# 64 bytes of padding ahead of two groups of SBUF tiles in a one-core transformer block

## The chip, the cores and the metric

The kernel runs on one core of one Trainium2 chip. The metric is the device time of one execution in microseconds (us); lower is better. A time given without more is the median of the runs shown.

## The reference, cut to what matters

One decoder layer on 2048 tokens with a model width of 1024, in float32: a mixer with eight dilated-attention heads beside a gated linear recurrence, and a squared-ReLU MLP, each between two RMS norms.

```
h = rms_norm(x, mix_norm_pre)
z = h @ w_in                                  # 1024 -> 2560: q, k, v, recurrence input, gate
m = concat(dilated_attention(q, k, v), rg_lru(conv(xr)) * gelu(gr)) @ w_out
x = x + rms_norm(m, mix_norm_post)
h = rms_norm(x, mlp_norm_pre)
x = x + rms_norm((relu(h @ w1) ** 2) @ w2, mlp_norm_post)   # 1024 -> 4096 -> 1024
```

## The kernel before, in words

Every large product is made in three TensorE passes. Each float32 operand is split into a high part (ScalarE rounds it to the faster fp32r type, L54) and a low part (the rest, by VectorE or GpSimd, L55), and a product is high x high, low x high and high x low. So every weight tile and every activation tile exists twice, with names that end in H and L. One such pass multiplies a 128 x 128 stationary operand by a 128 x 512 moving operand; the stationary operand of the next pass is loaded (LDWEIGHTS, engine PEld in the profile) while the current moving operand streams.

The tokens are worked in two halves of 1024. The order in time is:

- **w_in (L192 to L345, about 0 to 640 us of the profile).** `Project.product` (L193 to L202) makes one 128 x 512 block z of h @ w_in by 8 x 3 passes; there are 80 such blocks. The moving operands are the tiles hH and hL (h^T, eight each for each of two blocks of 512 tokens, numbered 0 and 1). The stationary operands are wH and wL, "w_in's parts". For the first four column tiles of w_in these come from a pool of their own ("x0"), for all the others from the pool "p1", in which hH, hL and the small norm tiles lie too. The attention of the first half (L368 to L741) and the recurrence run between these products.
- **Output projection (`OutProj`, L836 to L897)** for one half; in between, `Factors.columns` (L945 to L968) transposes the normed rows to h2^T on TensorE.
- **mlp_in (L1035 to L1167).** h2^T @ w1 by a two-level scheme with seven products instead of eight: products 1 to 7 each take one factor of w1 (tiles f_1 to f_7, stationary) and one factor of h2^T (moving). Product m of a pair j of w1's column tiles is 4 x 3 = 12 passes (L1070 to L1073), and there are 16 pairs in each half. `RIGHT` (L907) says which factor of h2^T a product takes. `Factors.EARLY` are the tiles B11 (product 1), B21 (product 2) and T3 (product 7), six tiles with H and L; `Factors.LATE` are T2, T4, T1 and B22 (products 6, 4, 5, 3). The early tiles lie in the pool "hA" on the left side of SBUF, the late ones in the pool "hB" on the right. In the profile the tiles hHB11, hHB21 and hHB22 all show as hHB, and hHT1 to hHT4 as hHT; the factor f_m tells which product it is.
- **mlp_out (L1170 to L1330)** with the second half's attention woven in, then output projection, mlp_in and mlp_out of the second half.

The order on TensorE follows the program from the output projection on; before that a scheduler sets it. SBUF is laid out by pools that grow from the left or the right side; a tile that is larger or new moves what its pool allocates after it, and the pools beyond. Memory is used again by later pools, and a first write waits for the last use of what lay there before.

In the built program the places of the operands, in bytes modulo 128, are:

| moving operand | at | stationary operand | at |
|---|---|---|---|
| hH (all), hL (block 0, and k = 0, 1 of block 1) | 64 | wH, wL of the pool x0 (first 8 blocks z) | 64 |
| hL (k = 2 to 7 of block 1) | 0 | wH, wL of the pool p1 (other 72 blocks z) | 0 |
| early h2^T tiles (products 1, 2, 7) | 32 | f_1 to f_7 | 96 |
| late h2^T tiles (products 3, 4, 5, 6) | 96 | f_1 to f_7 | 96 |

Of the kernel before, what the change touches and what calls it, by code (L numbers as in the profile page):

```python
# [8 lines left out]
F32 = mybir.dt.float32  # L9
# [6 lines left out]
P = 128  # L16
# [41 lines left out]
def rsqrt_mean(nc, pool, ss, k, name, eps, e=None):  # L58

    v = e or nc.vector  # L60
    ms = pool.tile([P, k], F32, tag="rs_ms", bufs=2, name=f"ms_{name}")
    sd = pool.tile([P, k], F32, tag="rs_sd", bufs=2, name=f"sd_{name}")
    r0 = pool.tile([P, k], F32, tag="rs_r0", bufs=2, name=f"r0_{name}")
    t = pool.tile([P, k], F32, tag="rs_t", bufs=2, name=f"t_{name}")
    r = pool.tile([P, k], F32, tag="rs_r", bufs=4, name=f"r_{name}")
    nc.scalar.activation(out=sd, in_=ss, func=AF.Sqrt, scale=1.0 / D, bias=eps)
    v.tensor_scalar(out=ms, in0=ss, scalar1=-0.5 / D, scalar2=-0.5 * EPS, op0=ALU.mult, op1=ALU.add)
    nc.vector.reciprocal(out=r0, in_=sd)
    if k == 1 and e is None:
        v.scalar_tensor_tensor(out=t, in0=r0, scalar=ms, in1=r0, op0=ALU.mult, op1=ALU.mult)  # L70
    else:
        v.tensor_tensor(out=t, in0=r0, in1=ms, op=ALU.mult)
        v.tensor_tensor(out=t, in0=t, in1=r0, op=ALU.mult)
    if e is None:
        v.scalar_tensor_tensor(out=r, in0=t, scalar=1.5, in1=r0, op0=ALU.add, op1=ALU.mult)
    else:
        v.tensor_scalar(out=t, in0=t, scalar1=1.5, scalar2=None, op0=ALU.add)
        v.tensor_tensor(out=r, in0=t, in1=r0, op=ALU.mult)
    return r
# [7 lines left out]
class Project:  # L87


    def __init__(self, tc, p, pa, pl, bank, cst, scr, x, xT, g1, w_in):  # L90
        self.tc, self.nc, self.p, self.pa, self.bank, self.cst, self.scr = tc, tc.nc, p, pa, bank, cst, scr
        self.x, self.xT, self.w_in, self.pl, self.norm, self.ahead = x, xT, w_in, pl, {}, {}
        self.h, self.bc, self.lo = [None] * NBH, [None] * NBH, tc.nc.gpsimd
        self.g1 = p.tile([P, KT], F32, tag="g1", name="g1_sb")
        self.g1_d = g1
# [36 lines left out]
    def load_norm(self, tb, px=None):  # L132

        nc, p = self.nc, self.p
        n = TB // P
        parts = 1 if px else 2
        w = D // parts
        ss = p.tile([P, 2, n], F32, tag="ss", bufs=2, name=f"ss{tb}")
        for j in range(n):
            for i in range(parts):  # L140
                if px:
                    t = px.tile([P, D], F32, tag="xn", bufs=4, name=f"xn{tb}_{j}")
                else:
                    t = self.pa.tile([P, TB], F32, tag="t512", bufs=3, name=f"xn{tb}_{j}_{i}")
                nc.sync.dma_start(out=t, in_=self.x[tb * TB + j * P:tb * TB + (j + 1) * P, i * w:(i + 1) * w])
                nc.scalar.activation(out=t, in_=t, func=AF.Square, accum_out=ss[:, i, j:j + 1])
        if parts == 2:
            nc.vector.tensor_tensor(out=ss[:, 0, :], in0=ss[:, 0, :], in1=ss[:, 1, :], op=ALU.add)
        self.norm[tb] = rsqrt_mean(nc, p, ss[:, 0, :], n, f"x{tb}", self.cst["eps"], nc.gpsimd if px else None)
# [775 lines left out]
class Factors:  # L925
# [5 lines left out]
    def __init__(self, nc, sh, hf, pH):  # L931
        self.nc, self.sh, self.hf, self.H = nc, sh, hf, {}

        R = {k: sh.r(f"h2r{hf}_{k}", (P, KH, TB)) for k in ("12", "21", "11", "22")}
        self.R = [[R["11"], R["12"]], [R["21"], R["22"]]]
        self.tiles(pH, self.EARLY)

    def tiles(self, pH, names):
# [786 lines left out]
```

## Time and profile before

| what | us |
|---|---|
| median of 3 runs | 2245.89 |
| lowest and highest of them | 2237.49, 2253.74 |
| span of the profiled execution, first to last instruction | 2246.4 |
| TensorE (PE) busy in it | 2167.4 (96%) |
| VectorE (DVE) busy | 1506.9 (67%) |
| ScalarE (ACT) busy | 1230.9 (55%) |
| GpSimd (POOL) busy | 450.9 (20%) |

The profile has only the span for the execution that it recorded; what lies around the span is not shown. The span is 0.5 us above the median of the runs. A matmul's duration in the profile runs from its start to a modelled end and overlaps the next matmul, so durations of about 390 ns stand for passes that start about 230 ns apart; the starts in the timeline are the better clock. "Who waited for whom" lists idle time of an engine by what ended it. The chain of work that ended last is followed back from the end of the program, and its shares say on which engine the time was being set.

### The profile page before, as it was taken

How to read it: one execution, taken by the hardware profiler on the slowest of the kernel's cores; microseconds unless marked ns; L12 is line 12 of the kernel's file. 1: busy time of each engine (PE TensorE's matmuls, PEld its weight loads, DVE VectorE, ACT ScalarE, POOL GpSimd, SP SyncE). 2: the span in 40 equal slices, each digit the busy share in tenths (PEclk: the TensorE clock that was granted, in tenths of full speed). 3: DMA queues.
4: the chain of work that ended last, by engine and by line, in shares of the span. 5: the costliest groups of instructions: out<-in, count | busy, mean ns of one | idle time of the engine just before them, and what ended most of it. 6: DMA issues, size and time to landing. Idle time of an engine off the chain costs nothing.

```text
span 2246.4 us, 30767 instructions
## 1 busy us (share of the span) xinstructions
PE 2167.4 (96%) x10264; PEld 1774.6 (79%) x10264; DVE 1506.9 (67%) x2908; ACT 1230.9 (55%) x2489; POOL 450.9 (20%) x536
## 2 busy tenths in 40 slices
PE   8999999979999999999999999989999999999998
PEld 6678878767788788888788787778878888888887
DVE  6767465978648867675567676777766566646456
ACT  7646464655434555554666666754455555654442
POOL 5543414455223000000001111113200000000003
PEclk9999999999999999999999999999999999999999
DMA  8365684645974676878777777877553444776665
GB/s 286 100 190 176 179 242 145 183 153 163 319 255 161 221 286 242 301 265 309 223 216 221 211 237 221 234 228 225 181 189 126 169 139 164 275 236 191 193 196 179
DMA packets 224116, 473.51 MB, mean 211 GB/s; under 512 B 23428, under 2 KB 78756, under 8 KB 217684
## 3 DMA queue, kind: packets, MB, share of 16 engines
q1 hardware_dynamic: 195140, 337.52, 47.9%
q0 software_dynamic: 28816, 134.01, 16.9%
q8 instruction: 81, 1.33, 0.2%
q14 instruction: 79, 0.65, 0.1%
HBM read 337.09 MB, written 151.13 MB: 217 GB/s over the span
## 4 chain that ended last, share of the span: by engine, by line
PE 70%; DVE 10%; DMA 8%; ACT 4%; issue 3%; POOL 1%; SPq 1%; DVEq 0%; ACTq 0%; POOLq 0%
PE o L1221 8%; PE o L1222 8%; PE o L1223 8%; PE za L1072 4%; PE za L1071 4%; PE za L1073 4%; PE z L198 3%; PE z L199 3%; PE z L200 3%; PE m L858 3%; PE m L857 3%; PE m L859 3%; PE zc L1071 2%; PE zc L1072 2%; PE zc L1073 2%
## 5 line engine op out<-in xcount | busy, mean ns | idle before, releaser
L198 PE MATMUL z<-hH,wH 128*128 128x512 f32 x640 | 263.8, 412 | 15.4 <-ACT wH L54 5.7
L199 PE MATMUL z<-hL,wH 128*128 128x512 f32 x640 | 260.5, 407 | 0.3 <-DVE hL L173 0.3
L200 PE MATMUL z<-hH,wL 128*128 128x512 f32 x640 | 259.6, 407 | 0.5 <-DVE wL L55 0.5
L198 PEld LDWEIGHTS z<-hH,wH 128*128 128x128 f32 x640 | 122.9, 192 | 50.6 <-ACT wH L54 8.3
L199 PEld LDWEIGHTS z<-hL,wH 128*128 128x128 f32 x640 | 122.8, 192 | 31.2 <-issue 4.8
L200 PEld LDWEIGHTS z<-hH,wL 128*128 128x128 f32 x640 | 122.9, 192 | 30.6 <-issue 4.6
L420 ACT ACTIVATE smB<-smB,stB 128x128 f32<-128x128 f32 (+3 forms) x128 | 71.6, 560 | 90.5 <-DVE stB L414 90.2
L1076 ACT ACTIVATE sq<-sq 128x512 f32<-128x512 f32 x93 | 58.8, 632 | 92.1 <-DVE sq L1080 92.1
L55 POOL TENSOR_TENSOR wL<-wraw,wH 128x512 fp32r<-128x512 f32 x58 | 82.4, 1437 | 80.5 <-ACT wH L54 76.7
L55 DVE TENSOR_TENSOR tlB<-pT_B,thB 128x384 fp32r<-128x384 f32 x96 | 57.1, 599 | 50.4 <-ACT thB L54 47.5
L1136 POOL DMA_DIRECT2D sa<-sq x31 | 16.6, 534 | 363.9 <-ACT sq L1077 353.4
L54 ACT CAST wH<-wraw 128x512 fp32r<-128x512 f32 (+1 forms) x81 | 47.2, 612 | 65.5 <-DMA wraw<-in_dram 31.6
L420 ACT ACTIVATE sm<-sm,stA 128x256 f32<-128x256 f32 (+1 forms) x128 | 63.1, 495 | 30.3 <-DVE stA L414 29.9
L1077 ACT ACTIVATE sq<-sq 128x512 f32<-128x512 f32 x124 | 76.2, 629 | 1.8
L1255 POOL TENSOR_TENSOR y<-y,g4b 128x512 f32<-128x512 f32 x8 | 12.3, 1577 | 259.4 <-ACT junk_y L84 259.4
L414 DVE CUSTOM_DVE_ANT_0 smB<-SB,mask_b 128x128 f32<-128x128 f32 (+3 forms) x128 | 59.3, 483 | 5.7 <-PE pT_B L393 5.4
L55 DVE TENSOR_TENSOR tlA<-pT,thA 128x512 fp32r<-128x512 f32 (+1 forms) x64 | 42.4, 670 | 26.4 <-ACT thA L54 26.0
L54 ACT CAST thB<-pT_B 128x384 fp32r<-128x384 f32 x96 | 48.4, 509 | 17.8 <-PE pT_B L393 9.7
L393 PE MATMUL pT_B<-ident,smB 128*128 128x128 f32 x320 | 51.5, 276 | 2.5 <-DVE na L409 0.9
L414 DVE CUSTOM_DVE_ANT_0 sm<-S,mask_a 128x256 f32<-128x256 f32 (+1 forms) x128 | 47.5, 410 | 9.3 <-PE pT L393 4.0
L640 PE MATMUL oB<-thB,vb 128*128 128x256 f32 x192 | 46.6, 274 | 6.6 <-ACT thB L54 5.9
L1072 PE MATMUL za<-hLT,f_5H 128*128 128x512 f32 x128 | 50.0, 391 | 2.0 <-DVE hLT L55 2.0
(607 smaller groups left out, 7041.4 us busy)
## 6 DMA issues: line engine op xcount, KB each, us to landing
sa<-as POOLq DMA_DIRECT2D x31, 1024.0 KB, 6.2
w1r<-in_dram SPq DMA_DIRECT2D x56, 512.0 KB, 4.0
sa<-sq POOLq DMA_DIRECT2D x31, 768.0 KB, 4.0
wraw<-in_dram SPq DMA_DIRECT2D x79, 256.0 KB, 3.8
place<-in_dram SPq DMA_DIRECT2D x14, 1024.0 KB, 7.9
sb<-place POOLq DMA_DIRECT2D x14, 1024.0 KB, 5.3
kh<-sk SPq DMA_DIRECT2D x24, 512.0 KB, 5.0
kl<-sk SPq DMA_DIRECT2D x24, 512.0 KB, 7.1
```

The lines of the kernel that those rows point to most:

```text
L55: (lo_eng or nc.vector).tensor_tensor(out=lo, in0=src, in1=f32(hi), op=ALU.subtract))
L198: pe.matmul(z, hi[:, k, :], hh, start=(k == 0), stop=False)
L199: pe.matmul(z, hi[:, k, :], hl, start=False, stop=False)
L200: pe.matmul(z, lo[:, k, :], hh, start=False, stop=(k == KT - 1))
L414: v.tensor_tensor_reduce(out=sm[:, c0:c0 + w], in0=sp[:, c0:c0 + w], in1=mask[:, mask.shape[-1] - w:], scale=1.0, scalar=3.0e38, op0=ALU.a ...
L420: s.activation(out=sm[:, c0:c0 + w], in_=sm[:, c0:c0 + w], func=AF.Exp, scale=-1.0, bias=st[:, 0, u, cols[j]:cols[j] + 1], accum_out=st[:, ...
L1071: pe.matmul(o, hi[:, k], bh[:, k], start=start and k == 0, stop=False, skip_group_check=True)
L1072: pe.matmul(o, hi[:, k], bl[:, k], start=False, stop=False, skip_group_check=True)
L1073: pe.matmul(o, lo[:, k], bh[:, k], start=False, stop=k == KH - 1, skip_group_check=True)
L1221: pe.matmul(o, ah[:, ts], bh, start=fresh and j == 0, stop=False, skip_group_check=True)
L1222: pe.matmul(o, ah[:, ts], bl, start=False, stop=False, skip_group_check=True)
L1223: pe.matmul(o, al[:, ts], bh, start=False, stop=j == NJ - 1, skip_group_check=True)
```

## The change

Two edits. The tile `ss` (sums of squares, in the pool p1, two buffers) grows from 32 to 64 bytes for each partition, only its first half is used, and what p1 allocates after it moves up by 64 bytes. And a new tile of 64 bytes, written once by VectorE so that it exists, is allocated in the pool hA ahead of the early h2^T tiles, once in each half.

```
@@ -135,7 +135,7 @@
         n = TB // P
         parts = 1 if px else 2
         w = D // parts
-        ss = p.tile([P, 2, n], F32, tag="ss", bufs=2, name=f"ss{tb}")
+        ss = p.tile([P, 4, n], F32, tag="ss", bufs=2, name=f"ss{tb}")
         for j in range(n):
             for i in range(parts):
                 if px:
@@ -933,6 +933,7 @@
 
         R = {k: sh.r(f"h2r{hf}_{k}", (P, KH, TB)) for k in ("12", "21", "11", "22")}
         self.R = [[R["11"], R["12"]], [R["21"], R["22"]]]
+        nc.vector.memset(pH.tile([P, 16], F32, name=f"pad_h{hf}"), 0.0)
         self.tiles(pH, self.EARLY)
 
     def tiles(self, pH, names):
```

In the built program of the change, wH and wL of p1, and hL k = 2 to 7 of block 1, lie at 64 modulo 128 (hH stays at 64), and the early h2^T tiles at 96 (f stays at 96). All passes of w_in and mlp_in then have both operands at equal places. Before, 1536 of w_in's 1920 passes and 1152 of mlp_in's 2688 had them at unequal places; 216 of w_in's had both at 0. The recurrence's tiles behind p1 move from 64 to 0 together with their weights. The instructions of PE, ACT, POOL and SP keep their order; VectorE has two more. The first stands among the last splits of q, k and v of the second half (zl and vs: low parts of k and of v, zn: scaled z):

```order
 L228 TENSOR_TENSOR zn_11_1_6196<-z_11_1_6171,bc_3353 128x512
 L55 TENSOR_TENSOR vs_11_0_6167<-vt_11_0_6162,vs_11_0_6167 128x8x64
+L936 MEMSET pad_h_6273 128x16
 L55 TENSOR_TENSOR zl_7_0_6083<-zn_7_0_6080,zh_7_0_6082 128x512
 L55 TENSOR_TENSOR vs_11_1_6203<-vt_11_1_6198,vs_11_1_6203 128x8x64
 L55 TENSOR_TENSOR zl_7_1_6118<-zn_7_1_6115,zh_7_1_6117 128x512
```

Only the row with the + is new. The second stands on VectorE after the first finished row tile of the second half's output projection (xt: normed rows; nm_x, nm_m: small norm values; x: rows after the mixer); this is the change's order there:

```order
L818 SCALAR_TENSOR_TENSOR nm_x_14741<-nm_x_14741 128x1
L895 SCALAR_TENSOR_TENSOR xt_14680<-x_8_14744,nm_x_14741,g3b_0_14686 128x512
L895 SCALAR_TENSOR_TENSOR xt_14680<-x_8_14744,nm_x_14741,g3b_1_14687 128x512
L936 MEMSET pad_h_14668 128x16
L815 TENSOR_SCALAR nm_m_14830<-nm_m_14830 128x1
L816 RECIPROCAL nm_m_14830<-nm_m_14830 128x1
```

Again the memset is the only new row; neither memset waits on a semaphore. Because the early tiles sit 64 bytes higher, a few first writes in the second half wait for other former tenants: the first write of hHB21 (L54) now also waits for the store of the output rows y_6 of the first half (L1265), and the first write of hLB11 (L55) for that of y_4.

More of the change, by code (lines that the diff above doesn't have):

```diff
@@ L137, in load_norm @@
         w = D // parts
-        ss = p.tile([P, 2, n], F32, tag="ss", bufs=2, name=f"ss{tb}")
+        ss = p.tile([P, 4, n], F32, tag="ss", bufs=2, name=f"ss{tb}")
         for j in range(n):
@@ L935, in __init__ @@
         self.R = [[R["11"], R["12"]], [R["21"], R["22"]]]
+        nc.vector.memset(pH.tile([P, 16], F32, name=f"pad_h{hf}"), 0.0)
         self.tiles(pH, self.EARLY)
```

## The prediction

> **What bounds the kernel now.** I read the page first, for the engine that sets the end.
>
> ```profile
> span 2246.4 us, 30767 instructions
> PE 2167.4 (96%) x10264; PEld 1774.6 (79%) x10264; DVE 1506.9 (67%) x2908; ACT 1230.9 (55%) x2489; POOL 450.9 (20%) x536
> PE 70%; DVE 10%; DMA 8%; ACT 4%; issue 3%; POOL 1%; SPq 1%; DVEq 0%; ACTq 0%; POOLq 0%
> ```
>
> TensorE is busy nearly throughout, and 70% of the chain that ended last is its own work. The change takes no pass away. It can only change how long a pass takes, so I looked for passes of one shape that take different times. The instructions on the tiles hHB and hLT (durations are minimum, median, maximum in ns) show them:
>
> ```profile
> L1071 PE MATMUL za<-hHB,f_1H x128: 394/394/394, 730.4 to 1903.4; 128*128 128x512 f32 x128
> L1071 PE MATMUL zb<-hHB,f_2H x128: 394/394/478, 734.0 to 1906.2; 128*128 128x512 f32 x128
> L1071 PE MATMUL za<-hHB,f_3H x128: 389/389/389, 768.7 to 1930.9; 128*128 128x512 f32 x128
> L1072 PE MATMUL zc<-hLT,f_7H x128: 393/394/499, 750.1 to 1914.8; 128*128 128x512 f32 x128
> L1072 PE MATMUL zc<-hLT,f_4H x128: 389/389/397, 771.6 to 1933.9; 128*128 128x512 f32 x128
> ```
>
> The early products (f_1, f_2, f_7) take 394 ns and the late ones (f_3, f_4) 389, with no scatter to speak of: a property of the operands, not of the moment. Both kinds take f from the same pool and write the same kinds of PSUM bank; what differs is that the early moving tiles lie at 32 modulo 128 beside f at 96, and the late ones at 96. Durations end in a model, so I measure by starts. TensorE's timeline: start of an early product (zc, f_7) and of the product after it, then the same for a late one (za, f_5):
>
> ```profile
> 901.78 0.39 PE L1071 MATMUL zc<-hHT,f_7H 128*128 128x512 f32 x1
> ...
> 904.58 0.39 PE L1071 MATMUL za<-hHT,f_6H 128*128 128x512 f32 x1
> ...
> 915.58 0.39 PE L1071 MATMUL za<-hHT,f_5H 128*128 128x512 f32 x1
> ...
> 918.30 0.39 PE L1071 MATMUL za<-hHB,f_3H 128*128 128x512 f32 x1
> ```
>
> Twelve passes take 2.80 us when the places are unequal and 2.72 when they are equal: 0.08 us for a product, 6.7 ns for a pass. The same for w_in, 24 passes from a block's first row to the row after its last: one block with weights of pool x0 (both operands at 64), then four with weights of p1 (64 or 0 beside 0).
>
> ```profile
> 21.12 0.39 PE L198 MATMUL z<-hH,wH 128*128 128x512 f32 x1
> ...
> 26.57 0.39 PE L200 MATMUL z<-hH,wL 128*128 128x512 f32 x1
> ...
> 150.76 0.40 PE L198 MATMUL z<-hH,wH 128*128 128x512 f32 x1
> ...
> 156.36 0.40 PE L198 MATMUL z<-hH,wH 128*128 128x512 f32 x1
> ...
> 614.87 0.40 PE L198 MATMUL z<-hH,wH 128*128 128x512 f32 x1
> ...
> 620.38 0.39 PE L198 MATMUL z<-hH,wH 128*128 128x512 f32 x1
> ...
> 625.95 0.40 PE L198 MATMUL z<-hH,wH 128*128 128x512 f32 x1
> ...
> 631.45 0.39 PE L198 MATMUL z<-hH,wH 128*128 128x512 f32 x1
> ...
> 637.01 0.38 PE L240 MATMUL vt<-ident,zn 128*128 128x128 f32 x2
> ```
>
> 5.45 us for the equal block; 5.60, 5.51, 5.50 and 5.56 for the others, 0.05 to 0.15 more, 0.09 in the mean. The hH of the first block are the same kind of tiles at the same place as in the later ones, so it is not the moving operand's place alone.
>
> The Trainium skill ("TensorE: Matmul & The Clock Gate", section "Step-by-step: what each phase is for") speaks against this reading: it gives TensorE two independent SBUF read ports and says that loading the next weights takes no read bandwidth from the running matmul. By that, a common offset of the two operands should be worth nothing and the kernel should stay at 2246. The 394 against 389 ns above do not agree with it, and I go by them.
>
> **The change part by part.** Not every pass lies on the path that sets the end. The chain of work that ended last, by line, in three stretches: w_in and the first output projection, mlp_in of the first half, mlp_in of the second.
>
> ```profile
> by line: PE z L198 9.3%; PE z L199 9.0%; PE z L200 8.9%; issue 5.9%; PE m L858 3.9%; PE m L857 3.9%; PE m L859 3.9%; DVE xc L310 3.0%; DVE xc L331 2.2%; DMA xr<-in_dram 1.4%; DMA sw<-in_dram 1.3%; DMA woL<-swo 1.2%; DMA wraw<-in_dram 1.2%;
> ...
> by line: PE za L1072 11.9%; PE za L1071 11.8%; PE za L1073 11.7%; DMA w2x<-in_dram 8.2%; PE zc L1071 6.5%; PE zc L1072 6.4%; PE zc L1073 6.3%; issue 5.4%; DMA sa<-sq 3.1%; DMA w1r<-in_dram 2.7%; PE zb L1073 2.7%; PE zb L1071 2.6%; PE zb L10
> ...
> by line: PE za L1072 17.2%; PE za L1073 17.1%; PE za L1071 17.0%; PE zc L1073 8.7%; PE zc L1072 8.7%; PE zc L1071 8.7%; PE zb L1071 3.8%; PE zb L1072 3.8%; PE zb L1073 3.8%; DVE hLT L55 2.5%; DMA w1r<-in_dram 1.8%; PE o L1222 1.2%; PE o L12
> ```
>
> *Early products.* The rows zb are product 2 alone, always an early one, and stand for all three. In the first half they hold some 8% of 317 us (741 to 1058), 25 us of the 16 x 2.80 = 45 us that the half's product 2 needs: 57% on the path. In the second, 11.4% of 316 us (1630 to 1946), 36 of 45: 80%. There are 48 early products in each half, so 27 + 38 = 65 count, times 0.08 us: **5.2 us**. The others are hidden: in the first half the chain leaves TensorE for the loads of w2x, which keep coming late, and at both starts for the split of the late tiles (hLT), so a product that is done sooner only lengthens the wait behind it. If all 96 counted it would be 7.7; nothing excludes a gain of 0 if the wait just moves.
>
> *w_in's parts.* The z rows hold 27.2% of the first 741 us, 202 us; at 5.54 us for a block (the mean of the four) that is 36 of the 72 blocks with weights of p1. The eight blocks with weights of x0 come first, and the chain's first piece is at 91.7 us (below), after them, so all 36 are blocks that change. At the mean of 0.09 this is 3.2, at 0.15, 5.4, at 0.05, 1.8; I take **3.3 us**, near the mean, as four blocks are a small sample. All 72 at 0.15 would be 10.8. The other half of the blocks runs beside VectorE and loads that end later:
>
> ```profile
> 91.71 0.85 issue
> ...
> 562.89 8.69 DMA woL<-swo
> 575.64 8.08 DMA er<-in_dram
> 596.87 8.63 DMA sq<-zl
> 605.62 0.70 DVE zl L55
> 606.42 0.70 DVE zn L228
> ```
>
> *The memsets.* The nearest rows are the kernel's own, of 128 and of 4 columns; the new ones have 16. The third row is the wait behind the second memset's place.
>
> ```profile
> L1471 DVE MEMSET ones<- x1: 165/165/165, 0.8 to 0.8; 128x128 f32 x1
> L287 DVE MEMSET state<- x1: 62/62/62, 1.0 to 1.0; 128x4 f32 x1
> ...
> 1551.62 0.16 DVE L816 RECIPROCAL nm_m<-nm_m 128x1 f32<-128x1 f32 x1 [1.01 <-ACT nm_m L814]
> ```
>
> So each costs 0.06 to 0.17 us, nearer the small one: 0.07. The first stands ahead of zl on VectorE, which is on the chain above, so it counts; behind it wait zl and the loads of zl's store. The second falls before a wait of VectorE for ScalarE and is covered by it; without that cover it would cost the same. Together **0.1 us** lost, 0.3 at most.
>
> *Sum.* 5.2 + 3.3 - 0.1 = 8.4 us off the profiled span of 2246.4, which is 2238.0. The median of the runs is 0.5 us below that span; from 2245.9 the sum gives **2237.5 us**.
>
> *Where the wait goes next.* In mlp_in of the first half the products reach the same loads sooner, so the waits of TensorE there should grow by up to the 21 hidden products' 1.7 us; in w_in by up to 36 x 0.09 = 3.2 us.
>
> **Rivals.**
>
> *All of it arrives.* If the loads and splits that now end the waits are themselves released by TensorE's earlier work, they move with it, and every pass counts: 7.7 + 72 x 0.09 = 14.2, so **2232 us**. For it: most loads wait for a buffer that a product frees. Against it: the chain's long DMA pieces above, whose length does not shrink.
>
> *w_in gives nothing.* The differences there are small and uneven (5.50 to 5.60), and half the path is others' work; a VectorE that is always a little late would absorb the rest. Then only the 5.2 remain: **2241 us**. Against it: 36 blocks stand on the chain without a wait.
>
> *The places do not matter.* Early and late products differ in more than the place: the early ones come first in a pair, while factors of w1 are made. If that set the 394 ns, nothing changes: **2246 us**. Against it: in 128 passes the f_1H rows never leave 394, though the first two pairs load their factors ready-made. The Trainium skill's rule of two independent ports ("TensorE: Matmul & The Clock Gate", "Step-by-step: what each phase is for") would lead here.
>
> *Slower: a store that ScalarE now waits for.* The first write of hHB21 in the second half waits for the store of y_6, the third of the four at that place. Stores on L1265, ScalarE's first hHB casts, and what follows them on its queue:
>
> ```profile
> 1547.83 0.57 POOL L1265 DMA_DIRECT2D out_dram<-y  x1 [5.42 <-DMA y<-sx]
> DMA to landing us min/median/max: 4.7/5.3/10.8
> 1558.78 1.13 ACT L54 CAST hHB<-h2r 128x512 fp32r<-128x512 f32 x2
> 1561.46 0.60 ACT L882 ACTIVATE x<-m 128x512 f32<-128x512 f32 x1 [1.55 <-PE m L859]
> ```
>
> With the median 5.3 the store lands at 1553.1, 5.7 us before the cast. With the longest, 10.8, it lands at 1558.6, just in time. Only from there does it cost: queued behind the cast is L882, the square sum that the norm of the next row tile needs, with 1.55 us to spare, and after it TensorE's next output projection waits for the PSUM bank. To eat the 8.4 us gained it must land over 10 us late, 21 us after its issue, twice the longest of the eight; at 15 us late, 15 - 1.5 = 13.5 lost against 8.4 gained gives **2251 us**.
>
> **How the numbers follow.** The forecast has 0.60; all of it arrives 0.16; w_in gives nothing 0.10; no effect 0.10; the late store 0.04. The predicted time is the forecast's, 2237.5. Its own range is 2232 to 2243: the bounds of w_in (1.8 to 5.4) and some 3 us by which a median of three moves when single runs lie 16 us apart. The range for 8 in 10 goes down to 2229, past the first rival, and up to 2247, past no effect. A change of 1%, about what a measurement of this kernel can tell from none, is 22.5 us. Everything at its upper bound is 7.7 + 10.8 = 18.5, so faster by over 1% needs the first rival and a lucky set of runs as well: 0.06. Slower by over 1% needs the late store to be far later than any seen, or an unlucky set: 0.03. Within 1%: 0.91.
>
> **What would show it.** Right: in the profile after, the rows f_1, f_2 and f_7 at 389 ns like f_3 to f_6; every early product in 2.72 us; every undisturbed block z in 5.45; the memsets at about 70 ns; no longer wait of ScalarE before its first hHB casts of the second half. The gain by stretch: about 3 us by the end of w_in, 2 in the first mlp_in, 3 in the second. Wrong: early products still at 2.80, or blocks z still at 5.5 to 5.6, which would take away the mechanism; or passes that shrink as forecast while the waits on L198, L313 and L1071 grow by as much, which would leave the mechanism and take away the path shares; or a span that shrinks by 14 us or more.

## The result and the profile after

The change is faster by about a third of one per cent: over 22 runs each, the median goes from 2242.56 to 2235.83 us, and the ratio is 0.9969, with a 95% interval of 0.9958 to 0.9980. That is a gain of 7.0 us, between 4.5 and 9.4. The forecast was 8.4 us off, and 2237.5 us in all.

The page of the changed kernel: its span, the busy times of the engines and the chain that ended last by engine.

```profile
span 2233.4 us, 30770 instructions
PE 2155.4 (97%) x10264; PEld 1775.5 (79%) x10264; DVE 1507.1 (67%) x2910; ACT 1230.3 (55%) x2489; POOL 453.3 (20%) x536
PE 68%; DVE 12%; DMA 7%; ACT 4%; issue 3%; POOL 1%; SPq 1%; DVEq 0%; ACTq 0%; POOLq 0%
```

The number of matmuls is the same, 10264, and they are busy 12 us less, while the other engines hold what they had to within 3 us: nothing has been taken away, passes have become shorter. The two spans differ by 13.0 us, more than the medians. The changed kernel's profiled run took 2235.21 us, 1.8 more than its span; by the same 1.8 the profiled run of before took about 2248.2, 5.6 over the median of its 22 runs. So about 6 of the 13 us are scatter between two single executions, which no mechanism has to explain.

The instructions on hHB and hLT after the change (minimum, median and maximum in ns, as before; lines behind L936 are one higher now):

```profile
L1072 PE MATMUL za<-hHB,f_1H x128: 388/389/390, 725.4 to 1890.8; 128*128 128x512 f32 x128
L1072 PE MATMUL zb<-hHB,f_2H x128: 388/389/477, 728.9 to 1893.5; 128*128 128x512 f32 x128
L1072 PE MATMUL za<-hHB,f_3H x128: 388/389/390, 764.7 to 1917.9; 128*128 128x512 f32 x128
L1073 PE MATMUL zc<-hLT,f_7H x128: 387/389/504, 746.1 to 1901.9; 128*128 128x512 f32 x128
```

The early products f_1, f_2 and f_7, which stood at 393 to 394, are now at the 389 of the late ones. By starts, TensorE's timeline, first an early product (zc, f_7) and the product after it, then the last block z of w_in from its first row to the row after it:

```profile
895.29 0.39 PE L1072 MATMUL zc<-hHT,f_7H 128*128 128x512 f32 x1
...
898.01 0.39 PE L1072 MATMUL za<-hHT,f_6H 128*128 128x512 f32 x1
...
626.52 0.39 PE L198 MATMUL z<-hH,wH 128*128 128x512 f32 x1
...
631.97 0.60 PE L240 MATMUL vt<-ident,zn 128*128 128x128 f32 x4
```

2.72 us for the product and 5.45 for the block, as forecast. Over all 32 products of each kind the median from start to start falls from 2.800 to 2.720 us for products 1, 2 and 7 and stays at 2.720 for the others. The late product that follows an early one (f_6) had been at 2.740, since its first passes were slow too; it is at 2.720 now.

### The profile page after: what moved, and what is told of

It reads as the page before. It is cut to its first block, busy times and chain, and to the rows that moved or that the text cites. A ratio compares the mean times of both kernels' runs of the same rounds, so it can differ in the third digit from the quotient of the medians.

```text
span 2233.4 us, 30770 instructions
## 1 busy us (share of the span) xinstructions
PE 2155.4 (97%) x10264; PEld 1775.5 (79%) x10264; DVE 1507.1 (67%) x2910; ACT 1230.3 (55%) x2489; POOL 453.3 (20%) x536
## 4 chain that ended last, share of the span: by engine, by line
PE 68%; DVE 12%; DMA 7%; ACT 4%; issue 3%; POOL 1%; SPq 1%; DVEq 0%; ACTq 0%; POOLq 0%
PE o L1223 8%; PE o L1222 8%; PE o L1224 8%; PE za L1073 4%; PE za L1074 4%; PE za L1072 4%; PE z L198 3%; PE z L199 3%; PE z L200 3%; PE m L859 2%; PE m L858 2%; PE m L857 2%; PE zc L1073 2%; PE zc L1072 2%; PE zc L1074 2%
## 5 line engine op out<-in xcount | busy, mean ns | idle before, releaser
L55 POOL TENSOR_TENSOR wL<-wraw,wH 128x512 fp32r<-128x512 f32 x58 | 83.3, 1452 | 78.0 <-ACT wH L54 75.2
L55 DVE TENSOR_TENSOR tlB<-pT_B,thB 128x384 fp32r<-128x384 f32 x96 | 57.0, 598 | 51.6 <-ACT thB L54 48.7
L54 ACT CAST wH<-wraw 128x512 fp32r<-128x512 f32 (+1 forms) x81 | 47.2, 611 | 62.7 <-DMA wraw<-in_dram 31.9
L55 DVE TENSOR_TENSOR tlA<-pT,thA 128x512 fp32r<-128x512 f32 (+1 forms) x64 | 42.3, 669 | 26.1 <-ACT thA L54 25.8
L54 ACT CAST thB<-pT_B 128x384 fp32r<-128x384 f32 x96 | 48.4, 509 | 18.2 <-PE pT_B L393 10.8
L393 PE MATMUL pT_B<-ident,smB 128*128 128x128 f32 x320 | 52.3, 280 | 2.8 <-DVE nb L409 1.7
L1072 PE MATMUL zc<-hHT,f_7H 128*128 128x512 f32 x128 | 50.1, 391 | 2.8 <-ACT hHT L54 2.8
```

The costliest lines, as they stand in the source:

```text
L55: (lo_eng or nc.vector).tensor_tensor(out=lo, in0=src, in1=f32(hi), op=ALU.subtract))
L1072: pe.matmul(o, hi[:, k], bh[:, k], start=start and k == 0, stop=False, skip_group_check=True)
```

## The experiments

Product times below are medians over the 32 products of a kind, from the first pass's start to the start of the next product's first pass. "Offset" is the place of the moving operand less that of the stationary one, in bytes modulo 256; why 256 and not 128 comes out on the way. Where no ratio is given, the kernel ran once, and only these times were read. A mean start-to-start time is taken over "undisturbed" passes, those whose next pass starts less than 260 ns later.

### One part alone

The change has two edits. The first of the two kernels has only `ss` enlarged, the second only the tile ahead of the early h2^T.

```
e1_w_in_only:
-        ss = p.tile([P, 2, n], F32, tag="ss", bufs=2, name=f"ss{tb}")
+        ss = p.tile([P, 4, n], F32, tag="ss", bufs=2, name=f"ss{tb}")
e2_early_only:
+        nc.vector.memset(pH.tile([P, 16], F32, name=f"pad_h{hf}"), 0.0)
```

> Only the larger ss tile: wH, wL and the low hL at 64 modulo 128 like hH, the early h2^T tiles stay at 32 beside f at 96. Theory (equal places modulo 128 make a pass 4 to 7 ns shorter, and the chain says how many passes count): blocks z in 5.45 us where nothing disturbs them, early products still 2.80, and 3.3 us less than before, ratio 0.9985. Rival 'all of it arrives': 72 x 0.09 = 6.5 us less, ratio 0.997. Rival 'w_in gives nothing': blocks shorter, but waits on L198 and L313 longer by as much, ratio 1.000.

> Only the 64 bytes ahead of the early h2^T tiles; w_in's parts stay at 0. Theory: blocks z as before (5.50 to 5.60 us), early products in 2.72 us, 5.2 us less than before, ratio 0.9977. Rival 'all of it arrives': 7.7 us less, 0.9966. Rival 'the places do not matter': early products stay at 2.80, ratio 1.000.

w_in alone: 0.9986 (0.9973 to 0.9999), which is 3.1 us, between 0.2 and 6.1. The early tiles alone: 0.9975 (0.9964 to 0.9987), 5.6 us, between 2.9 and 8.1. The same row in the two kernels, w_in's padding first:

```profile
L1071 PE MATMUL za<-hHB,f_1H x128: 394/394/395, 724.8 to 1894.8; 128*128 128x512 f32 x128
```

```profile
L1072 PE MATMUL za<-hHB,f_1H x128: 389/389/390, 726.3 to 1891.7; 128*128 128x512 f32 x128
```

Each edit shortens its own passes and no others: with w_in's padding alone the undisturbed passes of w_in start 228.5 ns apart and products 1, 2 and 7 stay at 2.80 us, with the early tiles alone it is 230.8 ns and 2.72 us. The parts sum to 0.39%, and the whole gave 0.31% (0.20 to 0.42): they add up within what can be told.

### The late tiles moved off instead

All of the change, and the late tiles moved by 64 bytes, so that now these are at an offset from f:

```
-                    F.tiles(st.enter_context(sb(f"hB{hf}", "right")), F.LATE)
+                    pB = st.enter_context(sb(f"hB{hf}", "right"))
+                    F.tiles(pB, F.LATE)
+                    nc.vector.memset(pB.tile([P, 16], F32, name=f"pad_l{hf}"), 0.0)
```

> The change, and the late h2^T tiles moved down by 64 bytes to 32 modulo 128, f stays at 96; early tiles at 96. Theory: early products 2.72, late products now 2.80. 128 late products x 0.08 = 10.2 us, of which the path shares of the za rows (60% in the first half, 85% in the second) leave 7 to 8: the change's gain of 7 us is given back, ratio 0.999 to 1.001. Rival 'it is the side of SBUF or the place in the pair that sets the time': late products stay at 2.72, ratio 0.997 like the change.

The ratio is 1.0007 (0.9996 to 1.0018): the gain is gone. Early and late have changed places:

```profile
L1072 PE MATMUL za<-hHB,f_1H x128: 388/389/397, 728.0 to 1899.8; 128*128 128x512 f32 x128
L1072 PE MATMUL za<-hHB,f_3H x128: 393/394/398, 766.8 to 1927.6; 128*128 128x512 f32 x128
L1073 PE MATMUL za<-hLT,f_6H x128: 392/394/398, 753.7 to 1913.8; 128*128 128x512 f32 x128
```

Products 6 and 4 take 2.800 us, products 2 and 7 take 2.720 and 2.730. It is not that early products run beside the making of factors, nor anything about the tiles' side of SBUF: whichever group lies at another place than f is slow.

### The same equality at another place

Here the early tiles stay at 32 modulo 128, and 64 bytes at the end of the pool on the right move the factors and the late tiles to 32 as well; w_in's part as in the change.

```
+            nc.vector.memset(pg.tile([P, 16], F32, name="pad_g"), 0.0)
```

> The larger ss tile, no pad ahead of the early tiles; instead 64 bytes at the end of the right-hand pool of the factors, which moves f, the late tiles and w_out's parts from 96 to 32. The early tiles are not moved and are at 32, so both operands of all of mlp_in lie at 32. Theory (only equality counts): early and late products 2.72 us, ratio as the change's, 0.997. Rival '32 is a slow place for a moving operand': early stay at 2.80 and late go to 2.80, 3.3 us gained and 7 to 8 lost, ratio 1.002.

```profile
L1071 PE MATMUL za<-hHB,f_1H x128: 389/389/389, 723.2 to 1882.6; 128*128 128x512 f32 x128
L1071 PE MATMUL za<-hHB,f_3H x128: 389/389/390, 761.5 to 1909.8; 128*128 128x512 f32 x128
```

All seven products take 2.720 us, so no place is better than another by itself; equality is what counts. The ratio is 0.9956 (0.9938 to 0.9973). That is the lowest ratio of the study, but its interval overlaps the change's, and the passes are as long as in the change. Of the 8.6 us by which its profiled span is shorter than the change's, 5.4 lie between the end of the first half's mlp_in and the start of the second's: 566.7 us here, and 566.9 to 573.4 in the profiles of the other kernels; so it looks like scatter, though that is not shown.

### How equal: 32, 96 and 128 bytes apart

w_in's part as in the change; in each half the three early pairs stand at offsets of 32 (B11), 96 (B21) and 128 bytes (T3).

```
+            pair = []
+            for x in "HL":
+                n = {'HB11': 96, 'HB21': 64, 'HT3': 32}.get(x + b, 0)
+                if n:
+                    self.nc.vector.memset(pH.tile([P, n // 4], F32, name=f"pad{x}{b}_{self.hf}"), 0.0)
```

> The change with other paddings: moving tile minus f, modulo 512, is 32 bytes for B11 (product 1), 96 for B21 (product 2) and 128 for T3 (product 7); before it was 448 (64 modulo 128) for all three. Theory (modulo 128): products 1 and 2 slow, about 2.80 us for 12 passes or between 2.72 and 2.80, product 7 2.72. Rival 'the period is 64 bytes or another': with 64 as the period nothing but 32 and 96 could differ from 64, and 64 itself would have been fast, which it was not; with 256 or 512 product 7 would be slow, 2.80.

```profile
L1077 PE MATMUL za<-hHB,f_1H x128: 391/396/399, 726.4 to 1894.2; 128*128 128x512 f32 x128
L1077 PE MATMUL zb<-hHB,f_2H x128: 392/394/478, 730.0 to 1897.0; 128*128 128x512 f32 x128
L1078 PE MATMUL zc<-hLT,f_7H x128: 387/394/502, 746.2 to 1905.5; 128*128 128x512 f32 x128
```

```profile
897.13 0.40 PE L1077 MATMUL zc<-hHT,f_7H 128*128 128x512 f32 x1
...
899.93 0.39 PE L1077 MATMUL za<-hHT,f_6H 128*128 128x512 f32 x1
```

Product 7 lies at an equal place modulo 128 and takes 2.80 us all the same (the last two rows, of the timeline); the others 2.7995 and 2.798. Here the theory that equality modulo 128 is enough fell: a distance of 128 bytes is as bad as 32, 96 or the 192 of the kernel before. The change works because the pairs that it makes equal modulo 128 happen to be equal modulo 256 too.

### 256, 16 and 4 bytes apart

```
+        up = {"B11": 320, "B21": 16, "T3": 4}
...
+                    t = pH.tile([P, KH * TB + 32], F32R, tag=f"h{x}{b}", name=f"h{x}{b}_{self.hf}")
+                    i = up[b] // 4
+                    self.H[b].append(t[:, i:i + KH * TB].rearrange("p (k t) -> p k t", t=TB))
```

> As e5 with 256 bytes for B11, 16 for B21 (H; its low tile at 144, the same modulo 128) and 4 for T3 (H; its low tile at 132). Theory (modulo 128): product 1 2.72; products 2 and 7 not equal modulo 128, so slower, by how much is open (if lines of 32 or 64 bytes are what meets, 4 bytes cost nothing or very little). Rival 'period 512': product 1 at 2.80.

```profile
L1081 PE MATMUL za<-hHB,f_1H x128: 389/389/391, 725.4 to 1895.3; 128*128 128x512 f32 x128
L1081 PE MATMUL zc<-hHT,f_7H x128: 396/396/493, 744.2 to 1906.4; 128*128 128x512 f32 x128
```

256 bytes apart is as good as 0 (product 1: 2.721 us). Small distances help nothing: product 2 at 16 (its low part at 144, since the longer tile moved it) takes 2.772, product 7 at 4 (low part 132) 2.830, more than any larger distance.

### The change, and 128 bytes more

Both paddings 192 bytes instead of 64: everything that the change makes equal modulo 128 still is, and is 128 apart modulo 256.

```
+        ss = p.tile([P, 8, n], F32, tag="ss", bufs=2, name=f"ss{tb}")
...
+        nc.vector.memset(pH.tile([P, 48], F32, name=f"pad_h{hf}"), 0.0)
```

> The change with both paddings 128 bytes larger (192 in place of 64): every operand pair of w_in and mlp_in that the change made equal is still equal modulo 128, but now 128 apart modulo 256. Theory after the offset runs (equal modulo 256 counts): early products 2.80 us, blocks z 5.50 to 5.60, time as before, ratio 0.999 to 1.001. Rival (equal modulo 128 counts, the prediction's form of it): early 2.72, z 5.45, ratio 0.997 like the change.

The ratio is 1.0003 (0.9992 to 1.0014): no gain is left.

```profile
L1072 PE MATMUL za<-hHB,f_1H x128: 390/394/404, 726.1 to 1894.8; 128*128 128x512 f32 x128
L1072 PE MATMUL za<-hHB,f_3H x128: 389/389/390, 764.8 to 1922.2; 128*128 128x512 f32 x128
```

Products 1, 2 and 7 take 2.793, 2.800 and 2.798, and w_in's undisturbed passes (starts under 260 ns apart) 231.3 ns in the mean, against 230.9 before and 228.4 with the change. This is the whole kernel's answer to the question of the period: 256 bytes.

### The rest of the scale

w_in's part as in the change, the early pairs at offsets of 160, 224 and 64 bytes, in the same manner as at 32, 96 and 128:

```
+                n = {'HB11': 224, 'HB21': 64, 'HT3': 96}.get(x + b, 0)
```

> The remaining offsets of the sweep: moving minus f modulo 256 is 160 for product 1, 224 for product 2, 64 for product 7. Theory (equal modulo 256 or not, and no grades): all three 2.80 us. Rival (the cost depends on the distance): 2.80 for 64 as for 192, other values for 160 and 224.

```profile
L1077 PE MATMUL za<-hHB,f_1H x128: 388/394/400, 731.2 to 1899.1; 128*128 128x512 f32 x128
L1077 PE MATMUL zb<-hHB,f_2H x128: 393/396/481, 734.8 to 1901.9; 128*128 128x512 f32 x128
L1077 PE MATMUL zc<-hHT,f_7H x128: 387/395/505, 750.8 to 1910.3; 128*128 128x512 f32 x128
L1077 PE MATMUL za<-hHT,f_6H x128: 389/397/496, 756.9 to 1913.0; 128*128 128x512 f32 x128
```

160 and 224 give 2.806 and 2.803 us. 64 gives only 2.764, but the product behind it, f_6, whose own operands are equal, is then at 2.770, and its row shows it (397 ns in the median). The two together lose 2.764 + 2.770 - 2 x 2.720 = 0.094, and in the kernel before 0.100. So part of the loss can fall on the next product's starts, and products are best compared with what follows them.

The last kernel of the scale puts high and low parts of the early pairs both at 16, 8 and 4 bytes, ahead of which the change's 64 bytes stand:

```
+        up = {"B11": 16, "B21": 8, "T3": 4}
...
+            if b == "B11":
+                self.nc.vector.memset(pH.tile([P, 16], F32, name=f"pad_h{self.hf}"), 0.0)
```

> Offsets under 32 bytes, the same modulo 256 for the high and the low tile: moving minus f is 16 bytes for product 1, 8 for product 2, 4 for product 7. Theory (any offset that is not 0 modulo 256 pays the same 0.08 us): 2.80 for all three. Rival 1 (what has to agree is a line of 32 or 64 bytes): 2.72 for all three. Rival 2 (a start off a multiple of 32 bytes costs something by itself): over 2.80, as the 2.83 of the product that was 4 and 132 off suggests.

```profile
L1081 PE MATMUL za<-hHB,f_1H x128: 388/392/401, 724.9 to 1895.4; 128*128 128x512 f32 x128
L1081 PE MATMUL zb<-hHB,f_2H x128: 391/396/481, 728.5 to 1898.2; 128*128 128x512 f32 x128
L1081 PE MATMUL zc<-hHT,f_7H x128: 393/402/502, 744.3 to 1906.6; 128*128 128x512 f32 x128
```

2.782, 2.801 and 2.854 us: the loss does not shrink with the distance, and at 4 bytes it is 0.13 us instead of 0.08. The whole scale, product times in us (the first figures at 4 and 16 are those whose low part stood at 132 and 144):

| offset | 0 | 4 | 8 | 16 | 32 | 64 | 96 | 128 | 160 | 192 | 224 | 256 |
|---|---|---|---|---|---|---|---|---|---|---|---|---|
| product | 2.72 | 2.83, 2.85 | 2.80 | 2.77, 2.78 | 2.80 | 2.76 (and 0.05 on the next) | 2.80 | 2.80 | 2.81 | 2.80 | 2.80 | 2.72 |

### Which of the three passes pays

A product cycles through H x fH, L x fH, H x fL. Can one place be mended without the other? First attempt: product 1 with only L off by 64; product 2 was to have only H off, but its L came to lie at 128, which counts as off too.

```
+                n = {'HB11': 64, 'LB11': 64, 'LB21': 64}.get(x + b, 0)
```

> As the change, but for product 1 only the low moving tile is 64 off (H equal), for product 2 only the high one is (low equal), product 7 equal. Each k is three passes: high x high, low x high, high x low; moving tiles H, L, H, stationary always f at 96. Theory (a pass pays when its own moving operand is off from the weights that are loaded while it streams): product 1 pays in 4 of 12 passes, 2.72 + 0.027 = 2.747 us, product 2 in 8 of 12, 2.773 us, product 7 2.72. Rival 'a pass that follows a change of place pays too' (w_in before, blocks with hL at 0 between hH at 64, were no faster than those with all at 64): both about 2.80.

Product 1 takes 2.777 us, product 2 2.783 and product 7 (at 128) 2.795. Only the first of these says what was asked. The second attempt has L of product 2 at an equal place modulo 256:

```
+                n = {'HB11': 64, 'LB11': 64, 'LB21': 192, 'HT3': 0}.get(x + b, 0)
```

> As e7, whose product 2 and 7 were 128 apart modulo 256 without intent: product 1 has only the low moving tile off by 64 (high equal modulo 256), product 2 only the high one off by 64 (low equal modulo 256), product 7 all equal. Theory A (a pass pays by its own operands alone): 2.72 + 4/12 x 0.08 = 2.747 and 2.773, product 7 2.72. Theory B (in e7 product 1 took 2.777: a pass beside one that is off pays too): product 1 2.777 again, product 2 between 2.777 and 2.80, product 7 2.72.

Product 1 (one pass of three off) takes 2.775, product 2 (two of three off) 2.766, product 7 (all equal) 2.720. If each pass paid for itself, 6.7 ns a time, these would lose 0.027 and 0.053 us; they lose 0.055 and 0.046. So a pass at an offset costs its neighbour something too, and the mean start-to-start times by place in the cycle (229.9, 231.4 and 232.8 ns for product 1; 228.7, 233.5 and 229.2 for product 2; 226.7 when all are equal) show no pass that is left unharmed. Which pass it falls on, these two products do not settle. For a kernel the point is that mending H alone, two passes of three, is far from enough: with L left at 64 the product still loses 0.055 us, against 0.094, the next product's share counted, when all three passes are at 64, and 0.100 at 192 in the kernel before.

### The transposes' identity

In the built programs the passes of the output projection and of mlp_out have equal places modulo 256 already before the change, so nothing is left to gain there. If equality helps every matmul, the 568 transposes of attention (L393; `ident` is the moving operand, the tile that is transposed the stationary one) might gain too. These tiles lie at an offset of 160 from it; `ident` moves by 96 bytes, which makes it 0, and a second padding of 160 behind it moves the rest by 256 in all, so that the other tiles keep their places modulo 256.

```
+        nc.vector.memset(c.tile([P, 24], F32, name="pad_i"), 0.0)
...
+        nc.vector.memset(c.tile([P, 40], F32, name="pad_j"), 0.0)
```

> The change, and 96 bytes ahead of the identity and 160 behind it, so that the rest of the left side moves by 256 and keeps its offsets modulo 256; the identity (moving) and the attention's transposed tiles (stationary) then lie equal modulo 256 in 568 transposes of L393, before 160 apart. Theory (the rule holds for passes of 128 float32 columns too): these transposes start a few ns closer, about 109 to 106 ns, some 2 us over all of them, half on the path: ratio 0.9965 against before, hardly apart from the change's 0.997. Rival (a pass of 128 columns has its time set by the weight load, not by the stream): L393 unchanged in spacing and in mean duration, ratio 0.997.

The ratio is 0.9971 (0.9956 to 0.9985), the change's own. The transposes in the change, and with `ident` moved:

```profile
L393 PE MATMUL pT_B<-ident,smB x320: 269/273/435, 186.0 to 1468.5; 128*128 128x128 f32 x160
```

```profile
L393 PE MATMUL pT_B<-ident,smB x320: 270/272/435, 186.1 to 1470.3; 128*128 128x128 f32 x160
```

No difference: the transposes that follow one another without a gap (starts under 150 ns apart) start 112.7 ns apart in the mean in the change and 112.6 with `ident` moved. At an offset of 160 these float32 passes of 128 columns do not pay what the fp32r passes of 512 do; which of the two properties spares them was not tried. In the kernel before, the fp32r passes of 256 columns at L557 point to the length: those that follow each other within 200 ns start 121 ns apart in the mean at an offset of 128 and 126 at 0, so here too an offset costs nothing that can be seen. But their moving operand is strided, so this does not settle it.

## Why the prediction was right, point by point

**The passes.** That the places of the operands, and not the moment, set 394 against 389 ns was right: the groups exchanged their times when the late tiles were moved off. The rival "the places do not matter" fell with it. The Trainium skill ("TensorE: Matmul & The Clock Gate", "Step-by-step: what each phase is for") gives the moving and the stationary operand read ports of their own, by which no place should count; 2.76 to 2.85 against 2.72 us for the same twelve passes disagree, at every offset tried but 0 and 256.

**The reason given for it was half right.** "Equal modulo 128" was a reading of two places that could not tell 128 from 256: the 96 and 32 of the table were 192 apart modulo 256, and the change closes exactly that. Offsets of 128 (product 7) and the whole kernel at 128 showed the period to be 256. The number was not touched by this, since no pair of the change lies at 128; that was luck, as 128 bytes more of padding, which the reason as given would have allowed, leave no gain.

**Early products, 5.2 us.** By the edit alone 5.6 (2.9 to 8.1), of the 7.7 that 96 products at 0.08 would give. Stretch by stretch, mlp_in's length from its first to its last pass, in the profiles whose early products are all unequal by a multiple of 32 bytes, with the late ones equal (before, w_in alone, 128 bytes more, and the offsets of 32 to 128 and of 64 to 224), and in those whose products are all equal (after, early alone, all at 32, the identity too):

| early products | first half, us | second half, us |
|---|---|---|
| unequal | 316.0, 314.5, 313.8, 316.2, 314.2 | 314.0, 315.6, 313.3, 313.4, 313.8 |
| equal | 312.8, 312.1, 312.8, 313.3 | 310.5, 310.1, 309.9, 309.8 |

The means differ by 2.2 and 3.9 us; the forecast by shares of the chain was 27 x 0.08 = 2.2 and 38 x 0.08 = 3.0. That the first half gives less than the 3.8 of its 48 products and the second nearly all was the point of reading the chain by stretch, and it held. The second was set low: 3.9 is all that its 48 can give.

**Where the rest of the first half went.** The forecast had hidden products lengthen the wait behind them. TensorE's waits in mlp_in of the first half, in the kernel before and after the change (us in total, times, longest):

```profile
PE za L1071 <- ACT sq L1115: 1.3, 1, 1.3
PE za L1071 <- ACT sq L1110: 1.2, 1, 1.2
PE zc L1071 <- DVE sq L1080: 0.6, 1, 0.6
PE za L1072 <- DVE hLT L55: 0.4, 1, 0.4
PE zc L1071 <- ACT hHT L54: 0.2, 1, 0.2
PE zc L1072 <- DVE hLT L55: 0.2, 1, 0.2
```

```profile
PE zc L1072 <- ACT hHT L54: 1.7, 1, 1.7
PE za L1072 <- ACT sq L1116: 1.4, 1, 1.4
PE za L1072 <- ACT sq L1111: 1.2, 1, 1.2
PE za L1073 <- DVE hLT L55: 0.5, 1, 0.5
PE zc L1073 <- DVE hLT L55: 0.2, 1, 0.2
```

3.9 us become 5.0, against up to 1.7 more in the forecast. The growth is at the split of the late tiles (hHT, 0.2 to 1.7), which the forecast named, and not at the loads of w2x. In the nine profiles of the table above, these waits sum to 2.5 to 4.3 us where the early products are unequal and to 4.2 to 5.0 where they are equal, 3.3 and 4.6 in the mean. That is 1.3 us more, which with the 2.2 us by which the stretch is shorter makes 3.5 of the 3.8 that 48 products give. The wait for hHT takes 0.7 of the 1.3; it varies from 0.2 to 1.2 and from 0.7 to 1.7, so that the waits grow is better shown than which one grows.

**w_in, 3.3 us.** The edit alone gave 3.1 (0.2 to 6.1). The count of 36 blocks cannot be checked apart; the 0.09 for a block, from four blocks, was too high. (The prediction's rows hold a fifth, from 620.38 to 625.95; at 5.57 us it would have raised the mean to 0.10.) The undisturbed passes of w_in start 230.93 ns apart before and 228.42 after: 2.51 x 1920 passes is 4.8 us in all, 0.067 for each of the 72 blocks, and 36 of those are 2.4. The stretch to the end of w_in is no measure of it: in the profiled pair it ends 5.0 us earlier, but the kernel with the early tiles alone, whose w_in is as before, starts mlp_in at 726.3 us, earlier than four of the kernels whose w_in is mended (728.0 to 731.2). The forecast's "about 3 us by the end of w_in" was a sign that one profile cannot show.

**The memsets.** 0.07 us each was right:

```profile
L936 DVE MEMSET pad_h<- x2: 72/72/72, 633.9 to 1541.0; 128x16 f32 x2
```

**The late store** did not come about. The third store of the four, ScalarE's casts and the square sum behind them after the change:

```profile
1538.58 0.57 POOL L1266 DMA_DIRECT2D out_dram<-y  x1 [5.53 <-DMA y<-sx]
```

```profile
1549.73 1.13 ACT L54 CAST hHB<-h2r 128x512 fp32r<-128x512 f32 x2
1551.96 0.60 ACT L882 ACTIVATE x<-m 128x512 f32<-128x512 f32 x1 [1.09 <-PE m L859]
```

The cast still stands 11 us behind the store's issue with no idle time ahead of it.

**All of it arrives** (14.2 us) lies outside the interval of 4.5 to 9.4. **w_in gives nothing** (5.2 us) lies inside it; only the edit alone, whose interval ends just short of 1, speaks against it.

**The base.** The sum was 8.4 and the gain 7.0 by the ratio; the oversized block explains 0.9 of the difference. The absolute time, 2237.5 against 2235.8, was near for one more reason: the three runs that were known put the kernel before at 2245.9, and 22 runs at 2242.6, so the base was 3.3 too high, and the gain, 8.4 against the medians' 6.7, took 1.7 of that back. That the two errors partly cancelled is luck.

## What to carry to other kernels

Where passes of one shape take two times without scatter, compare the start addresses of their moving and stationary operands modulo 256: equal ones save 6.7 ns of 233 in mlp_in's dense stream of 128 x 512 fp32r passes and 2.5 of 231 in w_in's, and it costs only some bytes of padding. Check the equality in the built program and at 256, for all the operands that take turns, since equality modulo 128 alone gives nothing, and with two passes of three mended more than half of the loss stayed. What it is worth is the saving of a pass times the passes that the chain of waits shows on its path, stretch by stretch.

## What the runs showed of the hardware that was not expected

- The period is 256 bytes, and within it there is no better distance: 32 to 224 bytes in steps of 32 all lose about 0.08 us in twelve passes (at 64 half of it falls on the next product), 4 bytes 0.11 to 0.13.
- The loss is not one pass's own. In the kernel before, undisturbed passes of w_in start 228.1 ns apart when a pass and the next both have equal places, and 230.5 to 233.1 in all other cases, also when only the next is unequal (233.1 for an equal pass ahead of one at 64). It is not so at every offset: with 128 bytes more, an equal pass ahead of one at 128 takes 228.8 ns, hardly over its 228.0.
- In w_in the loss is smaller than in mlp_in, at the same offset too. Where two passes with an offset of 64 follow each other in w_in, they start 230.5 ns apart, and 231.8 at 128 (in the kernel with 128 bytes more), against 228.1 at 0: 2.4 and 3.7 ns lost. In mlp_in product 7 takes 231.2 ns a pass at 64 and 233.2 at 128, against 226.9 at 0: 4.3 and 6.3 lost. Why is open.
- What in the memory or in TensorE makes the period is not shown by any of these runs, only that it is there.
